# Cutting loads and stores differently in a Winograd convolution: where the row chunks of the first, sixth and seventh image pairs lie

## The chip, the cores and the metric

The kernel runs on one core of a Trainium2 chip. A core has five engines with their own instruction streams: TensorE (PE, matrix multiply), VectorE (DVE), ScalarE (ACT), GpSimd (POOL) and SyncE (SP). Here SyncE issues every transfer between the chip's main memory and the core's on-chip memory; 16 DMA engines carry the transfers out. The metric is the time of one execution on the device in microseconds. Before the change it is 126.92 us, the median of three runs (126.87 to 127.02).

## The reference

A 3x3 convolution with padding 1: 16 images of 64 channels, 64x64 pixels, into 128 output channels, all float32.

```python
batch, c_in, h, w, c_out = 16, 64, 64, 64, 128
x_pad = np.pad(x, ((0, 0), (0, 0), (1, 1), (1, 1)), mode='constant')
output[b, co] += weight[co, ci, kh, kw] * x_pad[b, ci, kh:kh+h, kw:kw+w]   # over ci, kh, kw
```

The input is 16.8 MB, the weights 0.3 MB and the output 33.6 MB. All of it has to cross the DMA engines once.

## The kernel before

Two images are one pair: 2 x 64 channels fill the 128 partitions of the on-chip memory, so there are eight pairs, `p` = 0 to 7. A row of an image is 64 x 4 = 256 bytes, and an image of one channel 16 KB. Rows are computed two at a time by a Winograd scheme in one direction: of two neighbouring output rows, one is (G21 on row 1, G0 on row -1) + U, the other (G01 on row 0, G2 on row 2) + U, where U is a product of G1 with the sum of two input rows. The sums are made by VectorE (first pair) or GpSimd; the inputs are cast to half precision by ScalarE; TensorE multiplies; VectorE adds U and writes float32 to an output buffer; SyncE stores a whole pair (4 MB) once its four blocks of 16 rows are done.

The loads. The first pair comes in two pieces, the other pairs whole (2 MB each):

```python
cuts = [(0, 18), (18, 34), (34, 50), (50, 64)]      # also the pieces in which ScalarE casts
...
def load(p):
    ...
    for lo, hi in [(0, 18), (18, H)] if p == 0 else [(0, H)]:
        keep(nc.sync.dma_start(xf[p][:, lo:hi, :], x_rows[128 * p : 128 * p + 128, lo:hi, :]))
...
for p in range(LATE):       # LATE = 7: seven pairs are loaded at once, the eighth after the third store
    load(p)
...
for n in range(1, 4):
    sums(nc.vector, 0, xf[0], RB * n, RB)     # row sums of the first pair, 16 input rows each
```

The main loop and the stores. `blk` counts blocks of 16 output rows. The sixth pair (`p == 5`) is stored in four pieces: its first image; 58 rows of its second; and the last six rows of the second, once for partitions 0 to 123 and once for 124 to 127. The last pair is stored by halves:

```python
for p in range(NP):                 # NP = 8
    ...
    for blk in range(4):
        ...                         # U, A and Bt groups on TensorE; adds on VectorE
        parts = {3: (0, 64)} if p < NP - 1 else {1: (0, 32), 3: (32, 64)}
        if blk in parts:
            lo, hi = parts[blk]
            src = ots[p].rearrange("p b j i c -> p b (j i) c")
            dst = out_pairs[p]
            if p == 5:
                keep(nc.sync.dma_start(dst[:, 0, :, :], src[:, 0, :, :]))
                keep(nc.sync.dma_start(dst[:, 1, 0:58, :], src[:, 1, 0:58, :]))
                for q0, q1 in ((0, 124), (124, 128)):
                    keep(nc.sync.dma_start(dst[q0:q1, 1, 58:64, :], src[q0:q1, 1, 58:64, :]))
            else:
                keep(nc.sync.dma_start(dst[:, :, lo:hi, :], src[:, :, lo:hi, :]))
            if p == 2:
                load(LATE)
```

Of the kernel before, what the change touches and what calls it, by code (L numbers as in the profile page):

```python
# [13 lines left out]
def kernel(  # L14
# [6 lines left out]
    nc = tc.nc  # L21
    B, CI, H, W = x.shape
    CO = weight.shape[0]
    assert H == 64 and W == 64 and CI == 64 and CO == 128 and B % 2 == 0
    NP = B // 2
    RB = 8

    keep = tc.keep_in_program_order
# [15 lines left out]
    def pair_slot(n, shape, name):  # L44
        return big.tile(shape, F32, tag=f"slot{n}", name=name)
# [3 lines left out]
    cuts = [(0, 18), (18, 34), (34, 50), (50, 64)]  # L49
# [4 lines left out]
    def load(p):  # L54
        if p >= 6:
            xf[p] = big.tile([128, H, W], F32, tag="single", name="xf")
        else:
            if p % 2 == 0:
                two[p // 2] = pair_slot(p // 2, [128, 2, H, W], "xf")
            xf[p] = two[p // 2][:, p % 2, :, :]  # L60
        for lo, hi in [(0, 18), (18, H)] if p == 0 else [(0, H)]:
            keep(
                nc.sync.dma_start(
                    xf[p][:, lo:hi, :], x_rows[128 * p : 128 * p + 128, lo:hi, :]
                )
            )
# [3 lines left out]
    def cast(p, n):  # L70
        if p not in xs:
            xs[p] = xpool.tile([128, H, W], F16, tag=f"xs{p % 4}", name="xs")
        lo, hi = cuts[n]
        copy = nc.gpsimd.tensor_copy if (p, n) in by_pool else nc.scalar.copy
        keep(copy(xs[p][:, lo:hi, :], xf[p][:, lo:hi, :]))  # L75
# [3 lines left out]
    def outs(p):  # L79
        ots[p] = pair_slot((p + 3) % 4, [128, 2, H // 2, 2, W], "ot")  # L80

    for p in range(LATE):
        load(p)
# [9 lines left out]
    def sums(eng, p, src, lo, n):  # L93
        if p not in ss:
            ss[p] = spool.tile([128, H // 2, W], F16, tag="ss", name="ss")
        v = src.rearrange("p (j i) c -> p j i c", i=2)
        keep(
            eng.tensor_add(  # L98
                ss[p][:, lo : lo + n, :], v[:, lo : lo + n, 0, :], v[:, lo : lo + n, 1, :]
            )  # L100
        )
# [34 lines left out]
    for p in range(NP):  # L136
        if p not in ots:
            outs(p)
        if p + 1 < NP:
            for lo in (0, 16):  # L140
                sums(nc.gpsimd, p + 1, xf[p + 1] if p in (0, 1, 6) else xs[p + 1], lo, 16)
            if p == 1 or p == 2:
                cast(2 * p + 1, 3)
        for blk in range(4):
            j0 = blk * RB

            def group(wi_rows):

                tiles = [
                    psum.tile([128, RB, W], F32, tag="acc", name="acc") for _ in range(2)  # L150
                ]
                n = 3 * len(wi_rows)
                i = 0
                for wi, off in wi_rows:
                    for kw in (1, 0, 2):
                        c_lo, c_hi = max(0, 1 - kw), min(W, W + 1 - kw)
                        for b2 in range(2):
                            p0 = 64 * b2
                            lo, hi = j0, j0 + RB
                            if off is None:  # L160
                                rhs = ss[p][p0 : p0 + 64, lo:hi, c_lo + kw - 1 : c_hi + kw - 1]
                            else:
                                while 2 * lo + off < 0:
                                    lo += 1
                                while 2 * (hi - 1) + off > H - 1:
                                    hi -= 1
                                first = 2 * lo + off
                                last = 2 * (hi - 1) + off
                                rhs = xs[p][
                                    p0 : p0 + 64,  # L170
                                    first : last + 1 : 2,
                                    c_lo + kw - 1 : c_hi + kw - 1,
                                ]
                            nc.tensor.matmul(  # L174
                                tiles[b2][:, lo - j0 : hi - j0, c_lo:c_hi],
                                Wt[p0 : p0 + 64, wi, kw, :],
                                rhs,
                                start=i == 0,
                                stop=i == n - 1,
                            )  # L180
                        i += 1
                return tiles

            U = group([(G1, None)])
            us = []
            for b2 in range(2):
                ut = upool.tile([128, RB, W], F32, tag="ut", name="ut")
                keep(nc.scalar.copy(ut, U[b2]))  # L188
                us.append(ut)
            for q, n in casts[p][blk]:  # L190
                cast(q, n)
            A = group([(G21, 1), (G0, -1)])
            for b2 in range(2):
                nc.vector.tensor_add(ots[p][:, b2, j0 : j0 + RB, 0, :], A[b2], us[b2])  # L194
            Bt = group([(G01, 0), (G2, 2)])
            for b2 in range(2):
                nc.vector.tensor_add(ots[p][:, b2, j0 : j0 + RB, 1, :], Bt[b2], us[b2])  # L197
            parts = {3: (0, 64)} if p < NP - 1 else {1: (0, 32), 3: (32, 64)}
            if blk in parts:
                lo, hi = parts[blk]  # L200
                src = ots[p].rearrange("p b j i c -> p b (j i) c")
                dst = out_pairs[p]
                if p == 5:

                    keep(nc.sync.dma_start(dst[:, 0, :, :], src[:, 0, :, :]))
                    keep(nc.sync.dma_start(dst[:, 1, 0:58, :], src[:, 1, 0:58, :]))
                    for q0, q1 in ((0, 124), (124, 128)):
                        keep(nc.sync.dma_start(dst[q0:q1, 1, 58:64, :], src[q0:q1, 1, 58:64, :]))
                else:
                    keep(nc.sync.dma_start(dst[:, :, lo:hi, :], src[:, :, lo:hi, :]))  # L210
                if p == 2:
                    load(LATE)
# [28 lines left out]
```

## Time and profile before

| | us | from |
|---|---|---|
| time of a run, median of three | 126.92 | the times |
| span of the profiled execution, first to last instruction | 125.1 | the page |
| TensorE busy | 106.0 | the page |
| VectorE busy | 84.0 | the page |
| ScalarE busy | 65.6 | the page |
| GpSimd busy | 33.4 | the page |
| first TensorE product of the convolution | 6.68 | the chain |
| last store issued (rows 32 to 63 of the last pair) | 112.76 | the DMA issues |
| last store landed, on the first and the last DMA engine | 120.8 and 124.2 | its completion events |

How to read the page: part 1 gives the busy time of each engine and its share of the span; part 2 cuts the span into 40 slices of 3.13 us and gives each a digit, the busy share in tenths; part 3 gives the DMA queues; part 4 follows back the chain of instructions that ended last. An engine that is idle while another is the limit costs nothing. In a table by stage, each engine has its busy time in that stretch and, in brackets, its number of instructions; the last three columns are the clock granted to TensorE (1.00 is full), the mean busy share of the 16 DMA engines, and the rate they moved in GB/s. The trace also has every single DMA packet with its start, duration and size, and the time of every completion event: each DMA engine that takes part in a transfer reports its own share.

### The profile page before, as it was taken

The page shows a single profiled execution, that of the slowest core. Times are in us where ns is not written, and L with a number is a line of the kernel's source. Part 1 is how long each engine was busy: PE and PEld are TensorE (multiplying, and loading weights), DVE is VectorE, ACT ScalarE, POOL GpSimd, SP SyncE. Part 2 cuts the span into 40 slices and gives each one's busy share as a digit, 9 for nine tenths or more (in the row PEclk, how much of TensorE's full clock was granted, in tenths as well). Part 3 has the DMA queues.
Part 4 walks back from the last instruction along what each step waited for, and adds up shares of the span by engine and source line. Part 5 has one row for each costly group of instructions (what it writes and reads, how often), then busy time and mean ns, then how long its engine had stood idle before and what let it go on. Part 6 is the DMA issues. An engine that isn't in the chain of part 4 may idle for free.

```text
span 125.1 us, 2426 instructions
## 1 busy us (share of the span) xinstructions
PE 106.0 (85%) x978; PEld 54.3 (43%) x978; DVE 84.0 (67%) x135; ACT 65.6 (52%) x98; POOL 33.4 (27%) x22
## 2 busy tenths in 40 slices
PE   0489999999999999999999999999999999960000
PEld 0334555545555455554555555455454555520000
DVE  0249977777777777777877787787888788770000
ACT  4283989998879896666433333333666633310000
POOL 2000395930790067005800490039100000000000
PEclk9999999999999999999999999999999999999655
DMA  4999999999999999999999999999999999999980
GB/s 123 326 442 430 430 424 424 451 430 419 424 430 424 432 427 440 424 419 424 424 440 435 430 424 419 430 419 440 445 419 423 432 413 430 416 414 430 432 341 34
DMA packets 4050, 50.77 MB, mean 406 GB/s; under 512 B 328, under 2 KB 456, under 8 KB 712
## 3 DMA queue, kind: packets, MB, share of 16 engines
q1 hardware_dynamic: 4040, 50.63, 96.1%
q8 instruction: 7, 0.11, 0.3%
q14 instruction: 3, 0.02, 0.0%
HBM read 17.07 MB, written 33.55 MB: 405 GB/s over the span
## 4 chain that ended last, share of the span: by engine, by line
PE 83%; DMA 4%; DVE 2%; issue 1%; DVEq 0%; SPq 0%
PE acc L174 83%; DMA xf<-in_x_dram 4%; DVE ot L194 1%; DVE ss L98 1%; DVEq L236 0%; DVE ot L197 0%; SPq L48 0%; DVEq L194 0%
## 5 line engine op out<-in xcount | busy, mean ns | idle before, releaser
L174 PE MATMUL acc<-xs,Wt 64*128 64x504 f16 (+3 forms) x768 | 88.8, 378 | 0.0
L174 PEld LDWEIGHTS <-Wt 64*128 64x128 f16 x960 | 53.2, 95 | 52.4 <-issue 3.2
L194 DVE TENSOR_TENSOR ot<-acc,ut 128x512 f32<-128x512 f32 x64 | 41.2, 686 | 21.1 <-PE acc L174 17.4
L188 ACT COPY ut<-acc 128x512 f32<-128x512 f32 x64 | 34.4, 590 | 39.5 <-issue 35.2
L197 DVE TENSOR_TENSOR ot<-acc,ut 128x512 f32<-128x512 f32 x64 | 41.1, 683 | 0.0
L75 ACT CAST xs<-xf 128x1024 f16<-128x1024 f32 (+2 forms) x30 | 30.9, 1064 | 0.8 <-DMA xf<-in_x_dram 0.8
L174 PE MATMUL acc<-ss,Wt 64*128 64x504 f16 (+1 forms) x192 | 27.0, 384 | 1.1 <-DVE ss L98 1.1
L98 POOL TENSOR_TENSOR ss<-xs 128x1024 f16<-128x1024 f16 x8 | 16.8, 2128 | 30.9 <-PE acc L174 30.9
L98 POOL TENSOR_TENSOR ss<-xf 128x1024 f16<-128x1024 f32 x6 | 14.1, 2371 | 23.2 <-DMA xf<-in_x_dram 13.3
L98 DVE TENSOR_TENSOR ss<-xf 128x512 f16<-128x512 f32 x4 | 2.6, 688 | 3.8 <-DMA xf<-in_x_dram 3.8
L116 PE MATMUL wp<-ident,w 128*64 128x128 f16 x18 | 1.3, 327 | 4.3 <-DVE w L88 4.3
L88 DVE CAST w<-w_raw 128x576 f16<-128x576 f32 x1 | 0.5, 460 | 3.7 <-DMA w_raw<-in_weight_dram 3.7
L116 PEld LDWEIGHTS <-w 128*64 128x64 f16 x18 | 1.1, 209 | 4.2 <-DVE w L88 4.2
L118 ACT CAST Wt<-wp 128x384 f16<-128x384 f32 x1 | 0.5, 479 | 2.9 <-PE wp L116 2.9
L75 POOL CAST xs<-xf 128x896 f16<-128x896 f32 x2 | 1.9, 944 | 0.0
L118 ACT ACT_TABLE_LOAD x1 | 1.3, 1283 | 0.7 <-PEq L225 0.7
L123 ACT CAST Wt<-wp 128x384 f16<-128x384 f32 x1 | 0.5, 478 | 0.5 <-DVE Wt L121 0.5
L120 DVE TENSOR_TENSOR Wt<-wp,Wt 128x384 f16<-128x384 f32 x1 | 0.6, 550 | 0.0
L121 DVE TENSOR_TENSOR Wt<-wp,Wt 128x384 f16<-128x384 f32 x1 | 0.5, 545 | 0.0
L124 ACT CAST Wt<-wp 128x384 f16<-128x384 f32 x1 | 0.5, 485 | 0.0
masks.py:199 POOL TENSOR_SCALAR_AFFINE_SELECT ident<-ident 128x128 f16<-128x128 f16 x1 | 0.3, 292 | 0.1
masks.py:197 POOL MEMSET ident<- 128x128 f16 x1 | 0.2, 204 | 0.3 <-POOLq L225 0.3
(4 smaller groups left out, 0.4 us busy)
## 6 DMA issues: line engine op xcount, KB each, us to landing
out_dram<-ot SPq DMA_DIRECT2D x6, 4096.0 KB, 20.3
xf<-in_x_dram SPq DMA_DIRECT2D x7, 2048.0 KB, 22.1
out_dram<-ot SPq DMA_DIRECT2D x3, 2048.0 KB, 13.0
out_dram<-ot SPq DMA_DIRECT2D x1, 1856.0 KB, 17.2
xf<-in_x_dram SPq DMA_DIRECT2D x1, 1472.0 KB
xf<-in_x_dram SPq DMA_DIRECT2D x1, 576.0 KB
w_raw<-in_weight_dram SPq DMA_DIRECT2D x1, 288.0 KB, 3.0
out_dram<-ot SPq DMA_DIRECT2D x1, 186.0 KB
```

Of the source, the lines that this page charges most:

```text
L75: keep(copy(xs[p][:, lo:hi, :], xf[p][:, lo:hi, :]))
L88: keep(nc.vector.tensor_copy(w16, w_raw))
L98: eng.tensor_add(ss[p][:, lo : lo + n, :], v[:, lo : lo + n, 0, :], v[:, lo : lo + n, 1, :])
L116: nc.tensor.matmul(wp[q : q + 64, k * CO : k * CO + CO], w16[:, t::9], ident)
L118: keep(nc.scalar.copy(wrow(G1), wps[1]))
L120: keep(nc.vector.tensor_sub(wrow(G21), wps[2], wrow(G1)))
L121: keep(nc.vector.tensor_sub(wrow(G01), wps[0], wrow(G1)))
L123: keep(nc.scalar.copy(wrow(G0), wps[0]))
L174: nc.tensor.matmul(tiles[b2][:, lo - j0 : hi - j0, c_lo:c_hi], Wt[p0 : p0 + 64, wi, kw, :], rhs, start=i == 0, stop=i == n - 1,)
L188: keep(nc.scalar.copy(ut, U[b2]))
L194: nc.vector.tensor_add(ots[p][:, b2, j0 : j0 + RB, 0, :], A[b2], us[b2])
L197: nc.vector.tensor_add(ots[p][:, b2, j0 : j0 + RB, 1, :], Bt[b2], us[b2])
```

## The change

Three cuts move. The computation, and the order of the instructions on TensorE, VectorE, ScalarE and GpSimd, stay as they are.

- The first pair is loaded in four row chunks (18, 16, 16 and 14 rows), those of the casts, in place of two (18 and 46). This lets the row sums and casts of the first pair begin as each chunk lands.
- The seventh pair is stored by halves, as the eighth already is, so that its first half can leave before its second is computed.
- The rows that are split off into stores of 124 and 4 partitions were the last six of the sixth pair's second image. They are now the last four of the sixth pair's and the last four of the seventh pair's second image. Such stores shift bytes between the 16 DMA engines.

```diff
-        for lo, hi in [(0, 18), (18, H)] if p == 0 else [(0, H)]:
+        for lo, hi in cuts if p == 0 else [(0, H)]:
...
-            parts = {3: (0, 64)} if p < NP - 1 else {1: (0, 32), 3: (32, 64)}
+            parts = {3: (0, 64)} if p < NP - 2 else {1: (0, 32), 3: (32, 64)}
...
-                if p == 5:
-
-                    keep(nc.sync.dma_start(dst[:, 0, :, :], src[:, 0, :, :]))
-                    keep(nc.sync.dma_start(dst[:, 1, 0:58, :], src[:, 1, 0:58, :]))
+                cut = 60 if p in (5, 6) and hi == H else hi
+                if cut == hi:
+                    keep(nc.sync.dma_start(dst[:, :, lo:hi, :], src[:, :, lo:hi, :]))
+                else:
+                    keep(nc.sync.dma_start(dst[:, 0, lo:hi, :], src[:, 0, lo:hi, :]))
+                    keep(nc.sync.dma_start(dst[:, 1, lo:cut, :], src[:, 1, lo:cut, :]))
                     for q0, q1 in ((0, 124), (124, 128)):
-                        keep(nc.sync.dma_start(dst[q0:q1, 1, 58:64, :], src[q0:q1, 1, 58:64, :]))
-                else:
-                    keep(nc.sync.dma_start(dst[:, :, lo:hi, :], src[:, :, lo:hi, :]))
+                        keep(nc.sync.dma_start(dst[q0:q1, 1, cut:hi, :], src[q0:q1, 1, cut:hi, :]))
```

## The prediction

> **What bounds the kernel now.** I read the busy table and the slices of the page first, then the DMA queue, then the chain, then the DMA issues in order of time, and last the record of single DMA packets. From the page:
>
> ```profile
> PE 106.0 (85%) x978; PEld 54.3 (43%) x978; DVE 84.0 (67%) x135; ACT 65.6 (52%) x98; POOL 33.4 (27%) x22
> ...
> PE   0489999999999999999999999999999999960000
> ...
> DMA  4999999999999999999999999999999999999980
> ...
> q1 hardware_dynamic: 4040, 50.63, 96.1%
> ...
> PE acc L174 83%; DMA xf<-in_x_dram 4%; DVE ot L194 1%; DVE ss L98 1%; DVEq L236 0%; DVE ot L197 0%; SPq L48 0%; DVEq L194 0%
> ```
>
> TensorE is busy 85%, but its digits fall to 0 four slices (12.5 us) before the end; the digits of the DMA engines stay at 9 to the last slices, and the one queue that carries all data fills 96.1% of 16 engines' time. The chain names TensorE because it follows instructions, and stops at the last store's predecessor. So I asked for the busy time by stage:
>
> ```profile
> 5.50:9.50 4.00, 2.88 (x16) 1.28 (x16) 1.62 (x3) 2.99 (x5) 0.00 (x0) 1.00 1.01 429
> 9.50:99.00 89.50, 89.50 (x834) 45.75 (x832) 70.99 (x114) 56.56 (x83) 32.65 (x16) 1.00 1.01 429
> 99.00:112.70 13.70, 12.37 (x116) 6.12 (x112) 10.94 (x18) 4.29 (x8) 0.00 (x0) 1.00 1.00 420
> 112.70:120.50 7.80, 0.00 (x0) 0.00 (x0) 0.03 (x1) 0.00 (x0) 0.00 (x0) 0.76 1.01 426
> 120.50:125.10 4.60, 0.00 (x0) 0.00 (x0) 0.00 (x0) 0.00 (x0) 0.00 (x0) 0.50 0.25 105
> ```
>
> The last two columns are the DMA share and GB/s. From 5.5 us to 120.5 us the 16 engines are full at 420 to 429 GB/s. Both TensorE and DMA are therefore full, but compute ends at 112.7 us, when the last 2 MB store is issued; at that time 2 MB of the store before it is still queued (it lands at 115.9 to 119.3 us, one time per DMA engine). The end is set by the **draining of the DMA engines**: the last store lands at 120.8 us on the first and 124.2 us on the last of them.
>
> Which engine is last, and why, I worked out from the packets (start, duration, size). They carry no engine number, but on an engine a packet starts 3 to 4 ns before the end of the one ahead, so 16 chains can be followed:
> - four engines that carry nothing but their share end at 120.5 to 120.7 us;
> - seven that each also take one 16 KB instruction fetch (0.9 us) end at 121.2 to 121.9;
> - four that carry the six split-off rows end at 121.98, 122.62, 122.69 and 123.30 (the last with two 8 KB fetches);
> - one **slow engine**, without the split rows, ends at 123.73: its 16 KB packets take about 644 ns while compute and stores run together, where all others take 611.
>
> **What the Trainium skill says.** "DMA: Bandwidth & Descriptors", section "Why a DMA increments its semaphore by 16 and not by 1": a DMA is split over the largest number of engines up to 16 that divides its outermost size, the lowest numbered first. So 124 and 4 partitions each use four engines, the same four. The trace agrees: the two small stores land with 4 increments that wait for data instead of 16, and 128 packets of 1536 bytes sit in four of the chains. The same page, "Why small descriptors are slow (HBM only)": there is a fixed cost per packet. The trace has it: 16384 B in 611 ns, 8192 in 309, so 302 ns for 8192 B (0.0369 ns per byte) and 7 ns fixed, about 4 net of the overlap; 1536 B take 65. The same page, "Latency and other measured facts", calls engines 7 and 15 usually slower, and guesses at a cause tied to stores issued by GpSimd; one slow engine is what I see, but on SyncE's queue. "Runtime: NRT & Kernel Launch", "Instruction fetch mechanics": instructions come in 16 KiB blocks on a queue of their own; the seven 16 KB packets on q8 agree. The TensorE program doesn't change, so I expect these fetches where they are.
>
> **The change, part by part.** The instruction lists of the compute engines are the same; only the DMA issues of SyncE change, 20 rows for 15. Each engine drains its own list, so I add up per engine.
>
> *First pair in four chunks (18, 16, 16, 14 rows) for two (18, 46).* Per engine 8 packets of 11776 B (441 ns) become 8 each of 4096, 4096 and 3584 B. By the line: 158 + 158 + 139 = 455 ns against 441, so +14 x 8 = +0.11 us, and two more completion packets at 6 ns net: **+0.12 us on every engine**, if small strided chunks run at the line. The gain meant is earlier data: VectorE waited 2.08 us for the second chunk. But the first TensorE wait is for chunk one, and TensorE ran 103.51 us without a break after 6.68 us, so nothing is gained there; and compute is not what ends last.
>
> *Seventh pair by halves.* Per engine 16 packets of 16384 B become 32 of 8192: 2 x 309 - 611 = 7 ns each, +0.11 us; with the extra completions **+0.12 us on every engine**. What it buys: the store of rows 0 to 31 can go at about 93.5 us, not 99.95. Before, the two earliest engines ran dry for 0.22 and 0.26 us at 100.9 us. Those end 3 us before the last, so this is hidden.
>
> *The rows moved.* Image 2 of the sixth pair gives up 4 rows instead of 6, the seventh pair gives up 4: 8 rows instead of 6. Twelve engines lose 2 rows x 256 B x 8 partitions = 4096 B, **-0.15 us** (-0.16 on the slow one). The four engines lose the same, but in place of 32 packets of 1536 B (62 ns net) they get 64 of 1024 B (by the line 45, net 42): 2.72 - 1.98 = +0.74 us, and two more completions: **+0.60 us**.
>
> *Sums.* Slow engine: 123.73 + 0.12 + 0.12 - 0.16 = 123.81. Latest of the four: 123.30 + 0.12 + 0.12 + 0.60 = 124.14. The maximum goes from 123.73 to 124.14: **+0.4 us**, and the bound passes from the slow engine to one of the four. 126.92 + 0.4 = 127.3 us.
>
> **The rivals.** *Strided chunks read slowly.* Chunk one of before, 128 pieces of 4608 B at 16 KB pitch, did not run at the line. Its packets took 267 ns in the mean, not 177, and from 3.4 to 4.8 us the engines together moved only 230 to 280 GB/s, against 429 once the 11776 B packets were alone:
>
> ```profile
> 3.00:5.50 2.50, 1.25 (x18) 1.13 (x19) 0.46 (x1) 0.48 (x1) 0.00 (x0) 1.00 1.06 314
> ```
>
> If that belongs to narrow slices of 16 KB rows, the next three chunks do the same: 1.47 MB at 250 GB/s is 5.9 us instead of 3.5, +2.4 us on every engine, 129.7 us in all; with engines out of step perhaps half of it, 128.5. For it: 11776 B packets beginning at 4.9 to 5.1 us were slowed much less than the 4608 B packets of the same moment, so the slowness goes with the slice and not with the time. Against: the first 4608 B packets ran at 175 to 178 ns with 13 engines already in the chunk.
>
> *SyncE's issuing disturbs the engines.* The slow stretch ends at 5.4 us, when SyncE has issued its last load, and its issues from 3.08 us on took 501 to 625 ns instead of 392 to 440. Two more issues of 0.45 us would lengthen the stretch by 1 us at some 60% of the rate: +0.4 us more, 127.7. Against: before 3.1 us it issued just as densely and the weights' 2304 B packets ran at their 93 ns.
>
> *The start is slow whatever is read.* Then only the sum above stands, 127.3.
>
> *The slow engine stays last or gains.* If it is slow per packet, and not per time or byte, doubling the packets of the seventh pair costs it up to 16 x 33 ns = 0.5 us more, 127.5; if packets of 8192 B escape (in the last stores, after compute had ended, they took 309 ns) it gains the same and ends at 123.3, and the four engines end last anyway.
>
> *A wait of compute takes over.* A first pair later by over 2 us delays the second pair: GpSimd's sums start at 14.58 us as it lands and take 4.70, and TensorE needs the first half of them at about 19.5. There are 2.4 us to spare for that half, and at the end the last store has some 3 us of queue ahead of it. So I give this nothing.
>
> **Range and chances.** I give the plain sum and the issue rival together about 60%, the slow strided chunks 40%, with +0.4 + 1.1 to 2.4 us there. The median lies a little above the plain sum, at 127.5 us; 8 times in 10 between 126.8 and 129.2. Over 2% slower would be 129.46 and needs the strided rival at nearly full size: 0.11. Nothing gives 2% faster; 0.01.
>
> **What would show it.** Right: stores draining with the DMA slices at 9 to the end, TensorE at zero some four slices before it; the four increments of the small stores later, and the last store's last landing about 0.4 us later on one of the four engines; 4096 B packets at about 158 ns. The strided rival: 4096 B packets at 250 to 300 ns, under 300 GB/s up to 9 us or more, and every landing from the second pair on late by 1 to 2.4 us. The issue rival: slow packets up to 6.4 us, whatever their size. Wrong altogether: a last landing before 123.7 us, a TensorE wait in the middle, or an idle stretch of the DMA engines.

## The result

The changed kernel takes 127.44 us (median of six runs, 127.36 to 128.14) against 126.93 us; the ratio is 1.0049, 95% interval 1.0025 to 1.0073. It is slower by about 0.6 us (0.3 to 0.9), half a per cent: inside the 2% that was called the same, and inside the range of 126.8 to 129.2.

The page of the changed kernel, the lines that answer to those of before:

```profile
PE 105.3 (84%) x978; PEld 54.0 (43%) x978; DVE 84.1 (67%) x135; ACT 65.5 (52%) x98; POOL 33.5 (27%) x22
...
PE   0479999999999999999999999999999999930000
...
DMA  4999999999999999999999999999999999999970
...
q1 hardware_dynamic: 4752, 50.63, 96.1%
...
PE acc L174 82%; DMA xf<-in_x_dram 4%; DVE ot L194 1%; DVE ss L98 1%; DVE ot L197 0%; DVEq L238 0%; SPq L48 0%; DVEq L194 0%
```

The picture is that of before. The same 50.63 MB go over the same queue, in 4752 packets instead of 4040; the DMA digits stay at 9 to the last slices. TensorE's last busy slice shows 3 where it showed 6: compute ends earlier, and the kernel later. The stages of the changed kernel (us, busy time and count of each engine, TensorE's clock, DMA share, GB/s; a packet counts where it starts, so a share can pass 1):

```profile
3.00:5.50 2.50, 1.31 (x18) 1.23 (x19) 0.46 (x1) 0.48 (x1) 0.00 (x0) 1.00 0.98 262
5.50:9.50 4.00, 2.58 (x14) 1.07 (x15) 2.91 (x5) 2.82 (x5) 0.00 (x0) 1.00 1.09 439
9.50:99.00 89.50, 89.50 (x841) 45.81 (x839) 70.26 (x113) 56.86 (x85) 32.79 (x16) 1.00 1.00 427
99.00:112.70 13.70, 11.90 (x112) 5.90 (x108) 10.49 (x17) 4.10 (x8) 0.00 (x0) 1.00 1.01 420
112.70:120.50 7.80, 0.00 (x0) 0.00 (x0) 0.00 (x0) 0.00 (x0) 0.00 (x0) 0.68 1.01 427
120.50:125.60 5.10, 0.00 (x0) 0.00 (x0) 0.00 (x0) 0.00 (x0) 0.00 (x0) 0.50 0.30 125
```

From 5.5 to 120.5 us the engines are as full as before. What is new is in the last line: 125 GB/s over 5.1 us instead of 105 over 4.6, more bytes that drain late. SyncE's issues of the last third (start, length, line, number of transfers):

```profile
87.23 1.18 SPq L212 DMA_DIRECT2D out_dram<-ot  x2
93.03 0.40 SPq L207 DMA_DIRECT2D out_dram<-ot  x1
98.88 0.36 SPq L209 DMA_DIRECT2D out_dram<-ot  x1
99.48 1.02 SPq L210 DMA_DIRECT2D out_dram<-ot  x1
100.55 1.19 SPq L212 DMA_DIRECT2D out_dram<-ot  x2
105.84 6.85 SPq L207 DMA_DIRECT2D out_dram<-ot  x2
```

The seventh pair's first half goes at 93.03 us, and its second in four pieces from 98.88 us on. The last store is issued at 112.29 us, 0.47 us earlier than before, and lands last at 124.50 us, 0.34 us later than before.

The packets, followed as 16 chains as in the prediction (where two engines take long packets at the same moment the chains can be exchanged, the end times can't):

| end of the chain, us | before | after | predicted |
|---|---|---|---|
| four engines with nothing extra | 120.50 to 120.71 | 120.10 to 120.84 | |
| seven with a 16 KB instruction fetch | 121.22 to 121.92 | 121.36 to 122.62 | |
| the four with split-off rows | 121.98, 122.62, 122.69, 123.30 | 122.84, 122.95, 123.49, 124.16 | latest 124.14 |
| the slow engine | 123.73 | 123.74 | 123.81 |

The bound has passed from the slow engine to one of the four. From the sum alone this could be luck in two terms; the parts, each run by itself, decide.

### The profile page after: what moved, and what is told of

It is laid out like the page before. It is cut to its first block, busy times and chain, and to the rows that moved or that the text cites. A ratio compares the mean times of both kernels' runs of the same rounds, so it can differ in the third digit from the quotient of the medians.

```text
span 125.6 us, 2434 instructions
## 1 busy us (share of the span) xinstructions
PE 105.3 (84%) x978; PEld 54.0 (43%) x978; DVE 84.1 (67%) x135; ACT 65.5 (52%) x98; POOL 33.5 (27%) x22
## 3 DMA queue, kind: packets, MB, share of 16 engines
q1 hardware_dynamic: 4752, 50.63, 96.1%
## 4 chain that ended last, share of the span: by engine, by line
PE 82%; DMA 4%; DVE 2%; issue 1%; DVEq 0%; SPq 0%
PE acc L174 82%; DMA xf<-in_x_dram 4%; DVE ot L194 1%; DVE ss L98 1%; DVE ot L197 0%; DVEq L238 0%; SPq L48 0%; DVEq L194 0%
```

## The experiments

The theory: every DMA engine drains its own list, and the kernel ends with the latest of them; compute is not the end. The rivals: the start pays for the chunks; the slow engine is slow per packet; only the sum of all bytes counts; SyncE's issuing slows the start. The ratios are to the kernel before, with 95% intervals; 0.001 is 0.13 us.

**The four chunks alone.**

```diff
-        for lo, hi in [(0, 18), (18, H)] if p == 0 else [(0, H)]:
+        for lo, hi in cuts if p == 0 else [(0, H)]:
```

> The kernel before with only the first pair's four chunks. Theory (each DMA engine drains its own list, the end is the latest of them): +0.12 us on every engine, the slow engine stays last, 127.05 us, ratio 1.001. Rival (the start pays for the chunks, the stores nothing): the whole change, about 127.4 us, ratio 1.004 to 1.005. In both the last store is issued about 0.5 us earlier than before, as in the changed kernel, and that buys nothing.

Measured: 127.25 us, ratio 1.0033 (1.0018 to 1.0048), +0.42 us (0.23 to 0.61). Neither number: the theory's +0.12 us is too small, and the rival's whole change too large for the centre, though its lower end is inside. The mechanism holds in the profile: the slow engine is last, at 124.49 us, with the four at 124.07 or less. The start is where it pays. The profile of this kernel early on:

```profile
3.00:5.50 2.50, 1.05 (x18) 1.05 (x18) 0.46 (x1) 0.40 (x1) 0.00 (x0) 1.00 0.94 283
5.50:8.00 2.50, 1.34 (x12) 0.65 (x10) 1.83 (x4) 1.40 (x3) 0.00 (x0) 1.00 1.01 367
```

and of the kernel before in the second stretch:

```profile
5.50:8.00 2.50, 1.38 (x10) 0.65 (x10) 1.62 (x3) 1.56 (x3) 0.00 (x0) 1.00 0.97 410
```

The engines are busy all the time and move 367 GB/s instead of 410: the packets are longer. The 4096 B packets took 177 ns in the mean where the shortest took 159. The expected earlier end of compute did not come in this profile (last store issued at 113.36 us); in the changed kernel it did (112.29), and the end came later all the same.

**The stores alone** (the changed kernel, first pair in two chunks):

```diff
-        for lo, hi in cuts if p == 0 else [(0, H)]:
+        for lo, hi in [(0, 18), (18, H)] if p == 0 else [(0, H)]:
```

> The changed kernel with the first pair in two chunks again: only the stores are changed. Theory: the four engines with the split rows are last, at 124.14 - 0.12 = 124.02 us, 127.2 to 127.3 us, ratio 1.002 to 1.003. Rival (the start pays): 126.9 us, ratio 1.000.

Measured: 127.28 us, ratio 1.0034 (1.0017 to 1.0050). As the theory has it. One of the four is last, at 124.39 us, the slow engine at 123.71; of the 124.39, 0.27 us is one 16 KB packet that took 885 ns at 69.5 us in this execution, without which it is 124.11 against 124.02 expected. So the start does not pay for everything: the stores alone cost as much as the chunks alone, and both together (1.0049) less than the sum of both (1.0067). By the theory they should add up in full, since the chunks burden every engine alike; the intervals don't part the two.

**The halves alone.**

```diff
-            parts = {3: (0, 64)} if p < NP - 1 else {1: (0, 32), 3: (32, 64)}
+            parts = {3: (0, 64)} if p < NP - 2 else {1: (0, 32), 3: (32, 64)}
```

> The kernel before with the seventh pair stored by halves, six rows split off as before. Theory: +0.12 us on every engine, slow engine last, 127.05 us, ratio 1.001. Rival (the slow engine is slow per packet): up to +0.5 us more, 127.5, ratio 1.005. Rival (8 KB packets escape the slowness): the four engines last at 123.4, 126.6 us, ratio 0.998.

Measured: 126.93 us, ratio 1.0007 (0.9984 to 1.0029). It excludes the one rival's 1.005 and, narrowly, the other's 0.998; the slow engine was last at 123.77 us (123.85 by the sum), one of the four next at 123.40. That the engine is slow per packet has fallen: it would have ended at 124.3.

**The rows alone.**

```diff
-                if p == 5:
+                if p in (5, 6):
...
-                    keep(nc.sync.dma_start(dst[:, 1, 0:58, :], src[:, 1, 0:58, :]))
+                    keep(nc.sync.dma_start(dst[:, 1, 0:60, :], src[:, 1, 0:60, :]))
                     for q0, q1 in ((0, 124), (124, 128)):
-                        keep(nc.sync.dma_start(dst[q0:q1, 1, 58:64, :], src[q0:q1, 1, 58:64, :]))
+                        keep(nc.sync.dma_start(dst[q0:q1, 1, 60:64, :], src[q0:q1, 1, 60:64, :]))
```

> The kernel before with four rows each of the sixth and seventh pair split off in place of six of the sixth, the seventh pair in one go. Theory: slow engine 123.73 - 0.16 = 123.57, latest of the four 123.30 + 0.60 = 123.90 us, so +0.17, 127.1 us, ratio 1.0013, and the last chain is one with 1024 B packets. Rival (the slow engine alone sets the end): 126.75 us, ratio 0.999.

Measured: 127.05 us, ratio 1.0006 (0.9985 to 1.0028): the 127.1 expected, but the interval doesn't exclude the rival's 0.999. The chains do: one of the four is last at 124.39 us, where the rival has them play no part. The end itself is 0.49 us later than the 123.90 expected. A single 16 KB packet took 1139 ns at 36.4 us, 0.53 us too long, and would make up for that; but seven others took 746 to 1098 ns within 1 us of it, and at that time the chains can be exchanged, so that it was on this engine is not shown.

**No rows split off at all.**

```diff
-                if p == 5:
+                if False:
```

> The kernel before with the sixth pair stored in one go, nothing split off. Theory: each engine gets 12 KB back, +0.45 us; the four lose their 1.98 us of small packets; the slow engine is last at 123.73 + 0.46 = 124.2 us, 127.4 us, ratio 1.0035, and the first landing of the last store is one of the four. Rival (which engine is last does not matter, only the sum of bytes): 126.9 or less, ratio 1.000, as there are 3 fewer transfers.

Measured: 127.41 us, ratio 1.0044 (1.0032 to 1.0056), 127.4 expected. With 152 fewer packets and three fewer transfers it is slower, so the sum of the work does not set the end. The last stage of this profile:

```profile
112.70:120.50 7.80, 0.00 (x0) 0.00 (x0) 0.00 (x0) 0.00 (x0) 0.00 (x0) 0.73 1.00 425
120.50:126.40 5.90, 0.00 (x0) 0.00 (x0) 0.00 (x0) 0.00 (x0) 0.00 (x0) 0.50 0.19 82
```

The mean of the last stretch (which reaches past the end of the kernel) is only 82 GB/s: 15 engines end by 122.55 us, and one, the slow one, works on alone to 124.07.

**Twelve rows split off, twice as many.**

```diff
-                    keep(nc.sync.dma_start(dst[:, 1, 0:58, :], src[:, 1, 0:58, :]))
+                    keep(nc.sync.dma_start(dst[:, 1, 0:52, :], src[:, 1, 0:52, :]))
                     for q0, q1 in ((0, 124), (124, 128)):
-                        keep(nc.sync.dma_start(dst[q0:q1, 1, 58:64, :], src[q0:q1, 1, 58:64, :]))
+                        keep(nc.sync.dma_start(dst[q0:q1, 1, 52:64, :], src[q0:q1, 1, 52:64, :]))
```

> The kernel before with twelve rows split off in place of six, in the same stores of 124 and 4 partitions. Theory: the four engines take 32 packets of 3072 B (120 ns) for 8 x 3072 B; the latest of them goes from 121.9 us without a split to 121.9 + 3.75 - 0.91 = 124.7 us, the slow engine from 124.07 to 123.15, so the four set the end and the time is 127.5 us, ratio 1.0045: as slow as no split, from the other side. Rival (the split helps because it relieves the slow engine, the more the better): 126.4 us, ratio 0.996.

Measured: 127.90 us, ratio 1.0068 (1.0054 to 1.0082). The four are last, at 123.47, 123.57, 123.98 and 124.80 us, with 121 ns for each 3072 B packet: 124.7 was expected. The time written beside it, 127.5, was a slip: 124.7 is 0.97 us after 123.73, which makes 127.9. So the time over the number of split rows is a V: 127.41 with none (slow engine last), 126.95 with six, 127.90 with twelve (the four last). Six is near its bottom.

```profile
112.70:120.50 7.80, 0.00 (x0) 0.00 (x0) 0.00 (x0) 0.00 (x0) 0.00 (x0) 0.74 0.99 420
120.50:126.40 5.90, 0.00 (x0) 0.00 (x0) 0.00 (x0) 0.00 (x0) 0.00 (x0) 0.50 0.27 114
```

In the same stretch as above 114 GB/s are left instead of 82: now the four and the slow engine (123.36 us) drain late.

**Relieve one engine only.** If the slow engine were the sixteenth, a store of 120 partitions, on 15 engines, would take rows from it alone, with more to gain than any split above.

```diff
-                    keep(nc.sync.dma_start(dst[:, 1, 0:58, :], src[:, 1, 0:58, :]))
+                    keep(nc.sync.dma_start(dst[:, 1, 0:36, :], src[:, 1, 0:36, :]))
-                    for q0, q1 in ((0, 124), (124, 128)):
-                        keep(nc.sync.dma_start(dst[q0:q1, 1, 58:64, :], src[q0:q1, 1, 58:64, :]))
+                    for q0, q1 in ((0, 120), (120, 124), (124, 128)):
+                        keep(nc.sync.dma_start(dst[q0:q1, 1, 36:64, :], src[q0:q1, 1, 36:64, :]))
```

> The kernel before with 28 rows of the sixth pair's second image split into stores of 120, 4 and 4 partitions, in place of six into 124 and 4. 120 partitions should go on 15 engines, so that only the sixteenth is relieved, by 28 x 256 x 8 = 57 KB (2.1 us), and its rows go to the four. Theory, if the slow engine is the sixteenth: slow engine 124.2 - 2.2 = 122.0, the four 121.7 + 0.54 = 122.2, engines with an instruction fetch 122.4 last: about 1.3 us less than before, 125.6 us, ratio 0.990. If the slow engine is another one: it ends at 124.2, 127.4 us, ratio 1.0035, and the chain with fewer packets is not the slow one. Rival (the engines' sum of bytes sets the end): ratio 1.000.

Measured: 127.66 us, ratio 1.0060 (1.0037 to 1.0082). 15 completion events waited for data, so the store did run on 15 engines, but the slow engine was one of them: its chain has six packets of 7168 B at 276 to 298 ns where most took 272. The hoped-for version has fallen. And there was something nobody expected: the last two packets of this chain took 536 and over 700 ns, and at the same time those of one other engine up to 742 ns. These two engines, the slow one and its partner, landed last, at 124.86 and 125.26 us, and no other after 123.27. That would account for the 0.26 us above the 127.4 of the second branch; it was not tested by itself.

**Relieve the last nine.** 119 partitions should run on seven engines.

```diff
-                    keep(nc.sync.dma_start(dst[:, 1, 0:58, :], src[:, 1, 0:58, :]))
+                    keep(nc.sync.dma_start(dst[:, 1, 0:56, :], src[:, 1, 0:56, :]))
-                    for q0, q1 in ((0, 124), (124, 128)):
-                        keep(nc.sync.dma_start(dst[q0:q1, 1, 58:64, :], src[q0:q1, 1, 58:64, :]))
+                    for q0, q1 in ((0, 119), (119, 126), (126, 128)):
+                        keep(nc.sync.dma_start(dst[q0:q1, 1, 56:64, :], src[q0:q1, 1, 56:64, :]))
```

> The kernel before with eight rows of the sixth pair's second image split into stores of 119, 7 and 2 partitions, which should run on the first seven engines, in place of six rows into 124 and 4 on the first four. Theory: from the ends without a split, the seven take 18 packets of 2048 B for 8 x 2048 B, +0.83 us, and end at 122.7 us, or at 123.4 where one of them has an instruction fetch of 16 KB; the slow engine, if it is not among the first seven, loses 0.6 us and ends at 123.45. 126.6 to 126.7 us, ratio 0.997 to 0.998, faster than both kernels by a little. If the slow engine is one of the seven: 124.1 + 0.8 = 124.9, 127.7 us, ratio 1.006. Rival (only the sum of bytes counts): 126.9 us.

Measured: 128.16 us, ratio 1.0084 (1.0070 to 1.0097): the branch in which the slow engine is one of the seven, whose 124.9 us at the end make 128.1 (the 127.7 written there is the same slip as above). In the one profiled execution TensorE ran at about half its rate, and there the 16 packets of a whole store on the one engine that was slow there took 611 ns for the first eight and 615 to 634 for the others, instead of about 644; the kernel was run again for a profile at full rate:

> The kernel with 119, 7 and 2 partitions again, for a profile of an undisturbed execution. If the slow engine is one of the first seven, the chain that ends last is one with 18 packets of 2048 B, slow in the 16 KB stores (about 644 ns), and the 2048 B packets of the others take 84 ns. If two engines collide over the shifted partitions, a run of 2048 B packets takes 150 ns and more on two engines at the same time, and these end last, at about 125 us. 128.2 us in both.

Measured: 128.26 us, ratio 1.0097 (1.0065 to 1.0129). The chain that ends last, at 125.09 us, has 16 KB stores of 634 to 672 ns, then 18 packets of 2048 B (84 to 102 ns), and ends 2.2 us after the next. The collision has fallen for this kernel: 120 of the 128 packets took 84 ns, one took 184 and the other seven are those of the slow engine. So the slow engine is one of the seven that a store of 119 partitions uses, and not one of the four that a store of 124 uses, nor the one that a store of 120 leaves out. If stores always take the lowest numbered engines, as the Trainium skill says ("DMA: Bandwidth & Descriptors", "Why a DMA increments its semaphore by 16 and not by 1"), it is the fifth, sixth or seventh; the packets carry no engine number, so no run shows this.

**Does SyncE's issuing slow the start?** A memset makes the third load wait.

```diff
-            if p % 2 == 0:
+            if p % 2 == 0 and p // 2 not in two:
...
-    for p in range(LATE):
+    for p in range(2):
         load(p)
...
     sums(nc.vector, 0, xf[0], 0, RB)
+    two[1] = pair_slot(1, [128, 2, H, W], "xf")
+    keep(nc.vector.memset(two[1][:, 0, 0, 0:1], 0.0))
+    for p in range(2, LATE):
+        load(p)
```

> The kernel before with one added one-column memset of the third pair's buffer on VectorE after the first row sum, so that SyncE issues only the weights, the first pair and the second pair at the start and the other loads from about 6.7 us on. If SyncE's issuing slows the first chunk: its 4608 B packets fall from a mean of 267 to about 178 ns, all engines gain about 0.7 us, 126.2 us, ratio 0.9945. If the start is slow whatever is issued: mean about 267 ns, 126.9 us, ratio 1.000. The queue does not run dry in either (the second pair lands at about 14.5 us).

Measured: 126.98 us, ratio 1.0008 (1.0001 to 1.0016). SyncE issued nothing between 2.5 and 6.8 us, and the first chunk was as slow as ever: 259 ns a packet in the mean, and this stretch, against 314 GB/s before:

```profile
3.00:5.50 2.50, 1.29 (x18) 1.18 (x19) 0.46 (x1) 0.48 (x1) 0.00 (x0) 1.00 0.99 318
```

The issue rival has fallen for the first chunk. For the added cost of the four chunks it was asked separately, with both edits:

> The kernel before with the first pair in four chunks and the late issue of the third to seventh pair of the run before this one. If the four chunks cost more than their packet overhead because SyncE still issues while they run: the cost falls to about 0.1 us, 127.05 us, ratio 1.001. If it is in the chunks themselves: 127.25 us, ratio 1.003, and 4096 B packets again at a mean of 164 to 177 ns where the shortest take 159.

Measured: 127.08 us, ratio 1.0006 (0.9989 to 1.0024). The two halves of this answer disagree. The time is what the issue rival expected; the profile is what the other did: 4096 B packets at a mean of 173 ns, and the slow engine last at 124.05 us, 0.32 later than before. The interval meets that of the four chunks alone (from 1.0018), so it doesn't decide. Nor does the kernel with the late issue alone, which differs by the chunks only: in time the chunks cost nothing against it (1.0006 and 1.0008), while in the profiles the second pair lands 0.23 us later in the mean of its 16 completion events (at 14.17 us instead of 13.94).

**Eight chunks.**

```diff
-        for lo, hi in [(0, 18), (18, H)] if p == 0 else [(0, H)]:
+        for lo, hi in [(0, 18), (18, 25), (25, 32), (32, 39), (39, 46), (46, 52), (52, 58), (58, 64)] if p == 0 else [(0, H)]:
```

> The kernel before with the first pair in eight chunks: 18, four of 7 and three of 6 rows. If a chunk costs only its packets' fixed 7 ns and its completions: 48 more packets per engine than two chunks at 4 to 7 ns and six more completions, +0.25 to +0.4 us, 127.2 to 127.3 us, ratio 1.002 to 1.003, and 1792 B packets at 73 ns. If narrow chunks cost what the four chunks alone measured (0.3 to 0.4 us for two more): three times that, 127.9 to 128.2 us, ratio 1.008 to 1.010, with packets well above 73 ns in the mean.

Measured: 127.61 us, ratio 1.0054 (1.0038 to 1.0071), +0.69 us (0.48 to 0.90): between the two. Its packets in the profile, all but the first chunk's, and those of the others; time per engine:

| kernel | packets of rows 18 to 63, us per engine | by the median packets |
|---|---|---|
| two chunks (before, stores alone, late issue) | 3.61, 3.54, 3.55 | 8 x 441 ns = 3.53 |
| four chunks (after, alone, late issue) | 3.76, 3.99, 3.88 | 8 x (159 + 159 + 140) = 3.66 |
| eight chunks | 4.16 | 32 x 74 + 24 x 65 = 3.93 |

Two thirds of the eight chunks' extra packet time (0.40 of 0.59 us, from the means 3.57 and 4.16) are the fixed cost per packet, part of it hidden by the overlap. The rest is single packets that were stretched: in this kernel too the rate after the first chunk is below that of two chunks.

```profile
5.50:8.00 2.50, 0.73 (x7) 0.41 (x6) 1.35 (x3) 1.15 (x1) 0.00 (x0) 1.00 1.02 354
```

354 GB/s at full engines, against 410 for two chunks.

No version tried beat both kernels; the kernel before was the best of all, or not to be told from the best.

## Why the prediction was right

**What bounds the kernel: right.** The drain of the DMA engines sets the end. In the changed kernel compute ended 0.47 us earlier and the kernel later; over all the profiles with a span of 125 to 127 us the last store's issue lies between 112.3 and 114.0 us and does not order the times (with the halves alone it went at 113.70 us, and the time was 126.93).

**The sum per engine: right, with one term mis-sized and another counted too high.** The end went from 123.73 to 124.16 us against 124.14 predicted, from the slow engine to one of the four. The terms of the stores stood the test alone to some 0.1 or 0.2 us: packets of 1024 B took 46 ns in every case (45 by the line); the slow engine ended at 124.07 us with no split and 123.36 with twelve rows, where 124.2 and 123.15 were expected; and no split, six rows and twelve rows fell on the V that the same arithmetic draws. The mis-sized term is the first: "**+0.12 us on every engine**, if small strided chunks run at the line". Most of them did, with a median of 159 ns, but 69 of the 768 packets of 4096 B in three profiles took more than 163 ns, up to 552. Packets of four chunks took 3.88 us per engine in the mean of these profiles, of two 3.57: +0.31 us, and the run alone cost +0.42 us. The second pair says the same: in the mean of its 16 completion events it lands at 14.16 to 14.37 us with four chunks, and at 13.83 to 14.15 us in nine profiles with two, 0.27 us apart.

That the end came within 0.02 us of the sum is luck. The terms for the chunks and for the halves leave in the 3 to 4 ns by which packets overlap, which the sum takes off in the term of the rows: without them each is 0.06 to 0.07 us and not 0.12 (with the halves alone the slow engine ended 0.04 us later than before), and the last of the four should end at 124.03 us. The start of the changed kernel's profile made up for most of this: its second pair landed 0.16 us later than that of before. The plain sum of 127.3 us and the median of 127.5 us that was given bracket the measured 127.44. Three slips change nothing: 64 x 42 ns are 2.69 us, not 2.72; the three chunks of the strided rival are 1.51 MB and take 6.0 us at 250 GB/s, not 5.9; and SyncE issues 28 transfers for 22, not 20 for 15.

**Strided chunks read slowly: fell at the size given.** The 18-row chunk was slow again (296 ns), but the next, of the same pitch and narrower still, ran at 417 GB/s from 6.0 to 6.8 us in the changed kernel, with a median of 159 ns where 250 to 300 was the sign. What is left of the rival is the mis-sized term above, some 0.2 us beyond the sum instead of 1.1 to 2.4. A narrow slice alone does not make a slow read, then. The argument that had been held for the rival, that 11776 B packets suffered less at the same moment, was no proof: they begin at the end of the slow stretch.

**SyncE's issuing disturbs the engines: fell for the first chunk**, by the late issue. The argument against it had a misreading: 93 ns is the median of the weights' packets before, and 20 of the 128 took over 150 ns, up to 666. **The start is slow whatever is read: left standing, not shown**; every run begins with the weights and the 18-row chunk, whose 4608 B packets cost each engine 0.5 to 1.0 us more than the line in every profile, changed or not.

**The slow engine gains or loses by smaller packets: fell**, both ways. With the halves alone its 8 KB packets took 314 to 347 ns up to 112.4 us, for 309 at full rate: about half the stretch of a 16 KB packet, so it is slow by time or byte.

**A wait of compute takes over: fell**, as expected.

What stays open: why some packets of the narrow chunks after the first are stretched (164 to 177 ns in the mean for 159), and whether late issuing helps there. Of the 69 long ones 51 begin between 6.5 and 7.5 us, when no packet of the two chunks of before was stretched.

## What to carry to other kernels

When the digits of the DMA engines are 9 from start to end, find the engine that ends last before moving any transfer, for the kernel ends with it: follow the packets, or look at the spread of the 16 completion events of the last store (here 3.3 us). An earlier store, an earlier load or an earlier end of compute is then worth nothing, while every extra packet (7 ns, of which the overlap hides 3 to 4) and every row given to the wrong engine is paid. Stores of 124 and 4 partitions are a fine tool for such a balance and have an optimum; smaller pieces reach it at a higher price.

## What was not expected of the hardware

One engine is slow in every profile whose packets could be followed, on four chips, and only in stores while the compute engines run. In the kernel before its 16 KB stores take about 644 ns (mostly 634, 644, 653 and 662, steps of some 9 ns) from 40 to 68 and from 76 to 111 us; the load of the last pair between, at 69 to 75 us, runs at 611 ns, as do all loads before 36 us, and from some 112 us on stores run at about the full rate too (309 ns for 8192 B). That return follows TensorE's last product, and its time moves with it: product 110.9, 111.4, 111.6 and 112.3 us, first packets at full rate from 111.2, 112.1, 112.2 and 112.7 us (changed kernel, before, 119 partitions, halves alone). It costs this engine about 3.3 us (97 packets by 33 to 35 ns), and is the reason why a balance pays at all. The Trainium skill ("DMA: Bandwidth & Descriptors", "Latency and other measured facts") calls engines 7 and 15 usually slower and guesses at a cause in the descriptor rings of transfers issued from GpSimd. Here all transfers come from SyncE, and if stores take the lowest numbered engines the slow one is neither of these. The time of the slowness, and the 611 to 634 ns with TensorE at half its rate, point to something that goes on while TensorE runs: in the changed kernel ScalarE's last instruction ends at 109.5 us, TensorE's last product at 110.9, the slowness at 111.2 and VectorE's last instruction only at 112.3. What it is was not tried.

Single 16 KB packets of over 700 ns, with no instruction fetch near, come from about 36 to 39 us, as the first stores begin, in all but one of the profiles with a span of 125 to 127 us: two in that of before, six in that of the changed kernel, 14 of up to 1655 ns with the halves alone. What they take beyond 611 ns comes to between 0 and 4.5 us over the 16 engines together. A few tenths in one profiled execution are therefore noise, and the ratios of many runs were needed for verdicts.

In the store of 120 partitions, at 103 to 105 us, with other engines already in the next store, two engines' 7168 B packets took up to 742 ns instead of 272. One of the two was the slow engine.
